# A hybrid decoder step: six feed-forward blocks regrouped into five, with the sample stages moved to the front

## The chip, the cores and the metric

The kernel runs on one core of one Trainium2 chip. The metric is the device time of one execution in microseconds (us). Weights, inputs and outputs lie in HBM; the core has TensorE (PE in the profile, with PEld for the loading of its weights), VectorE (DVE), ScalarE (ACT), GpSimd (POOL), SyncE (SP, which issues all DMAs here) and 16 DMA engines.

## The reference, cut to what matters

One layer of a decoder for 2048 prompt tokens and 64 sample tokens (8 sequences of 8), model width 1024, all in float32. Prompt and samples share the weights, but not the keys: the samples attend to caches of their own.

```
h = rmsnorm(x, g_mix);  proj = h @ w_in              # q 512, k 128, v 128, u 512
attn: causal window of 128, 8 heads on 2 kv heads, ALiBi, sinks
      (samples: keys of cache_win_k/v and the new ones)
pool: d = windowed means of u (2, 4, 8, 16) - u;  y = d @ w_pool * pool_scale
x = x + concat(attn, pool) @ w_out
h = rmsnorm(x, g_cross); q = h @ w_cq
x = x + softmax(q mem_k / 16) mem_v @ w_co           # 4 heads, 256 memory tokens
      (samples: cache_mem_k, cache_mem_v)
h = rmsnorm(x, g_ffn)
x = x + square(relu(h @ w_up)) @ w_down              # hidden 4096
y = rmsnorm(x, g_final)
```

Returned are y for prompt and samples, and the new keys, values and pooling states.

## The kernel before

Activations are kept transposed: 128 partitions of channels, tokens along the columns, so a matmul has a 128 x 128 weight tile as the stationary operand and the tokens of one block as columns. Each float32 operand is split into a rounded high part and a low rest, and each product takes three matmuls (high x high, high x low, low x high): these are L280 to L282 in `dense`, and L111 to L113 in `mm3`.

After a prologue, which normalises the 256 memory tokens, makes the memory's keys and values and folds w_cq, w_co and the pooling weights into scratch tensors in DRAM (a_s, b_s, wo_s), the program goes through three rounds, `superblock(s, ...)`, here called stage 1 to 3. Each has two token blocks (`SBLOCKS`): 384 and 384, 384 and 384, 256 and 256 + 64. The last block carries the 64 sample tokens. In each stage:

- `dense` on "in" makes k, v, q and the pooling input u for the two blocks. The first chunks ("lead") run alone; the rest is interleaved by `mix` with the window attention (`attn`). In stage 1 the lead also holds four folds (`fold`), each with two stores to wo_s through `put_fold`.
- "wo" adds the output projection to x, which `load_x` has loaded anew into XT[0] and XT[1]; these two buffers serve attention as scratch in between. `Norm` squares x on ScalarE, adds the squares on GpSimd (L206), and sums over partitions with a matmul against ones (L214, in `fin`); `apply` scales (DVE), rounds (ACT) and subtracts (DVE and POOL in turn).
- `cross` does the memory attention by the folded weights, with 512 columns of memory as moving operand. In stage 3, `mix(cross(), sample_cross(), 1, 2)` runs the samples' own attention beside it; `load_split` loads and splits w_cq and w_co there. The samples' window attention (`attn_sample`, with cache inputs cvz, ckz and spool) also runs in stage 3.
- "B" adds the memory output to x and normalises for the feed-forward (`after_co`).
- Feed-forward: `up(g)` and `down(g)` for eight groups of 512 hidden channels. up has four chunks of 24 matmuls per block and group; down has eight chunks of 12 per block and group. up(g) and down(g - 1) alternate, so the hidden activations of two groups are live. At the end `norm1` starts the next stage's first norm beside down(6) and down(7), and `final` scales and stores y.

The order on the engines follows the program's text, moved about by the framework's scheduler within the dependencies, which are tracked by the region of a buffer that an instruction touches. The calls of `flush` set when the pieces of a norm are put between the chunks of matmuls. Weight tiles come through `Stream`: a DMA of 512 KB into a staging buffer (FS, six of them), a rounding copy on ACT into WS (L132) and a subtraction on DVE (L133); up to five tiles are prepared ahead. Activations sit in 16 slots of 4 x 384 columns (ACTS), handed out in turn: four for a normalised block, two each for q, d, pt and a hidden group of one block.

Of the kernel before, what the change touches and what calls it, by code (L numbers as in the profile page):

```python
# [14 lines left out]
P = 128  # L15
# [36 lines left out]
def kernel(ctx: ExitStack, tc: tile.TileContext, io, nW=12, nF=6, nT=8):  # L52
# [8 lines left out]
    ACTS = Slots([sb(f"act{i}", 4 * NB, F32R) for i in range(16)])  # L61
    WS = Slots([sb(f"w{i}", 1024, F32R) for i in range(nW)])
    FS = Slots([sb(f"f{i}", 1088) for i in range(nF)])
    TS = Slots([sb(f"t{i}", 400) for i in range(nT)])
    XT = [sb(f"x{i}", 3136) for i in range(2)]
# [4 lines left out]
    b_s = drp.tile([8, P, 1024], F32, name="b_s", tag="b_s")  # L70

# [167 lines left out]
    class Act:  # L239
        def __init__(self, n):  # L240
            self.n = n
            self.h = [ACTS.get(), ACTS.get()]
            self.l = [ACTS.get(), ACTS.get()]

# [6 lines left out]
        def free(self):  # L251
            ACTS.put(*self.h, *self.l)
            self.h = self.l = None
# [107 lines left out]
    def prologue():  # L361
# [10 lines left out]
        hm = Act(256)  # L372
# [21 lines left out]
        for name, dst in (("ck", io["mk"]), ("cv", io["mv"])):  # L394
            a = Act(256)
# [47 lines left out]
    def make_blks(s):  # L443
        blks = []
        off = 0
        for b, (t0, npr, ns) in enumerate(SBLOCKS[s]):
            bl = Blk()
            bl.s, bl.b, bl.t0, bl.np, bl.ns, bl.n, bl.off = s, b, t0, npr, ns, npr + ns, off
            off += npr
            bl.xt = XT[b]  # L450
            bl.x = (lambda bl: lambda k, c0=0, c1=None: bl.xt[:, 0:8 * bl.n].rearrange("p (k n) -> p k n", n=bl.n)[:, k, c0:bl.n if c1 is None else c1])(bl)
            blks.append(bl)
        return blks

    def norm1(bl, wait=2):
# [5 lines left out]
        else:  # L461
            xs = [FS.get() for _ in range(4)]
            for i in range(4):
                nc.sync.dma_start(xs[i][:, 0:2 * n], io["x"][:, 8 * bl.t0 + 2 * i * n:8 * bl.t0 + 2 * (i + 1) * n])
# [4 lines left out]
        def rest():  # L469
            nm.fin()  # L470
            bl.h1 = Act(n)
# [5 lines left out]
    def load_x(bl):  # L477
        nc.sync.dma_start(bl.xt[:, 0:8 * bl.n], io["x"][:, 8 * bl.t0:8 * (bl.t0 + bl.n)])

    def superblock(s, blks, nxt):  # L480
        last = s == 2
        smp = blks[1] if last else None
# [8 lines left out]
        for bl in blks:  # L491
            bl.q = [ACTS.get(), ACTS.get()]
# [3 lines left out]
        if last:  # L496
# [14 lines left out]
        def in_evac(c, b, ps):  # L511
            bl = blks[b]
            n = bl.n
            if c == 0:
                for kv in range(2):
# [7 lines left out]
                    if b == 1 and not last:  # L523
                        for hl in range(2):
                            i = 2 * kv + hl
                            nc.gpsimd.tensor_copy(kcar[:, i * P:i * P + P], f32(kz[kv][hl][:, P + npt - P:P + npt]))
                if smp is bl:
                    t = TS.get()
                    nc.vector.tensor_copy(t[:, 0:192], ps[:, bl.np - P:n])
                    nc.sync.dma_start(io["wkp"], t[:, 0:P])  # L530
# [6 lines left out]
            elif c == 1:  # L537
                nc.vector.tensor_copy(v32[:, bl.off:bl.off + n], ps[:, 0:n])
                if smp is bl:
# [798 lines left out]
```

## Time and profile before

| | us |
|---|---|
| median of 3 runs (lowest, highest) | 2630.92 (2629.46, 2634.61) |
| the profiled execution | 2637.38 |
| its span, first to last instruction | 2635.6 |
| TensorE busy | 2570.1 |
| VectorE, ScalarE, GpSimd busy | 1305.4, 982.7, 667.5 |
| moved by DMA | 244.76 MB, 93 GB/s on average |
| granted TensorE clock | 0.991 |

In the profile a line such as "L280 PE MATMUL mm<-act,w 128\*128 128x384 f32 x1856" is a group: the source line, the engine, the operation, output and inputs by the program's names, the shape, and the count. Durations of single matmuls overlap, since they are pipelined; their pace is read from start to start. A row of the stretches gives the length, the busy time of PE, PEld, DVE, ACT and POOL, each with the instructions that touch the stretch, then the granted clock as a share of full speed, the busy share of the DMA engines, and GB/s. In a timeline, brackets hold the idle time before an instruction and what ended it.

### The profile page before, as it was taken

The numbers are of one execution on the slowest core, as the hardware profiler recorded it, in microseconds if no ns is written. First come the engines' busy times: TensorE is split into PE (matmuls) and PEld (weight loads), VectorE is DVE, ScalarE is ACT, GpSimd is POOL, SyncE is SP. The second block draws the span as 40 slices with busy tenths as digits, with TensorE's granted clock in tenths as the row PEclk, the third lists the DMA queues.
The fourth block names the chain that finished last, engine by engine and source line by source line (L and its number), as shares of the span: only waits on it lengthen the run. The fifth ranks groups of instructions, "written<-read, shape, count | busy, mean of one in ns | idle before, by whom it ended". The sixth has DMA issues, their size and how long they took to land. (4 is left out here: it accounts for less than half of the span.)

```text
span 2635.6 us, 39262 instructions
## 1 busy us (share of the span) xinstructions
PE 2570.1 (98%) x15753; PEld 2462.3 (93%) x15753; DVE 1305.4 (50%) x2283; ACT 982.7 (37%) x1923; POOL 667.5 (25%) x723
## 2 busy tenths in 40 slices
PE   8999999999999999999999999999999999999998
PEld 8799989999999999897999999999999669999998
DVE  8667553533333367936353333334766646334334
ACT  6666342422222244824342222223354434322231
POOL 2215322411111153433241111113324214111111
PEclk9999999999999999999999999999999999999999
DMA  7833111111111123131111111112414573222210
GB/s 276 262 124 117 64 47 66 65 65 64 65 65 64 56 68 109 52 125 57 67 58 61 64 64 64 65 56 69 141 61 148 179 265 110 88 81 81 87 59 37
DMA packets 92539, 244.76 MB, mean 93 GB/s; under 512 B 16772, under 2 KB 31556, under 8 KB 91204
## 3 DMA queue, kind: packets, MB, share of 16 engines
q1 hardware_dynamic: 92356, 242.25, 26.9%
q8 instruction: 123, 2.02, 0.3%
q14 instruction: 60, 0.49, 0.1%
HBM read 219.53 MB, written 22.69 MB: 92 GB/s over the span
## 5 line engine op out<-in xcount | busy, mean ns | idle before, releaser
L280 PE MATMUL mm<-act,w 128*128 128x384 f32 (+2 forms) x2784 | 904.8, 325 | 2.6 <-ACT act L631 1.6
L281 PE MATMUL mm<-act,w 128*128 128x384 f32 (+2 forms) x2784 | 899.9, 323 | 7.0 <-DVE act L235 5.6
L282 PE MATMUL mm<-act,w 128*128 128x384 f32 (+2 forms) x2784 | 898.3, 323 | 1.2 <-DVE w L133 1.2
L132 ACT CAST w<-f 128x1024 fp32r<-128x1024 f32 x330 | 346.1, 1050 | 742.2 <-PE mm L112 457.4
L133 DVE TENSOR_TENSOR w<-f,w 128x1024 fp32r<-128x1024 f32 x330 | 423.5, 1289 | 305.8 <-ACT w L132 305.5
L111 PE MATMUL mm<-act,w 128*128 128x384 f32 (+2 forms) x1728 | 552.7, 320 | 9.2 <-ACT w L132 7.5
L113 PE MATMUL mm<-act,w 128*128 128x384 f32 (+2 forms) x1728 | 548.8, 318 | 0.5 <-DVE w L133 0.5
L112 PE MATMUL mm<-act,w 128*128 128x384 f32 (+2 forms) x1728 | 549.0, 318 | 0.0
L281 PEld LDWEIGHTS mm<-act,w 128*128 128x128 f32 x2784 | 528.3, 190 | 16.5 <-DVE act L235 7.3
L280 PEld LDWEIGHTS mm<-act,w 128*128 128x128 f32 x2784 | 528.4, 190 | 7.7 <-issue 3.0
L282 PEld LDWEIGHTS mm<-act,w 128*128 128x128 f32 x2784 | 528.0, 190 | 2.0 <-DVE w L133 1.8
L1131 POOL TENSOR_TENSOR t<-t 128x384 f32<-128x384 f32 (+2 forms) x192 | 218.1, 1136 | 1039.9 <-ACT t L1130 1039.9
L1164 DVE TENSOR_TENSOR x<-mm,x 128x384 f32<-128x384 f32 (+2 forms) x384 | 199.6, 522 | 325.3 <-PE mm L113 325.3
L111 PEld LDWEIGHTS mm<-act,w 128*128 128x128 f32 x1728 | 327.1, 189 | 10.9 <-ACT w L132 7.5
L112 PEld LDWEIGHTS mm<-act,w 128*128 128x128 f32 x1728 | 327.2, 189 | 1.2 <-issue 0.3
L113 PEld LDWEIGHTS mm<-act,w 128*128 128x128 f32 x1728 | 326.9, 189 | 0.8 <-DVE w L133 0.8
L206 POOL TENSOR_TENSOR t<-t,t 128x384 f32<-128x384 f32 (+2 forms) x161 | 192.8, 1198 | 348.6 <-ACT t L205 316.1
L1134 DVE TENSOR_TENSOR act<-t,act 128x384 fp32r<-128x384 f32 (+2 forms) x192 | 102.8, 535 | 301.2 <-ACT act L1133 301.2
L1133 ACT CAST act<-t 128x384 fp32r<-128x384 f32 (+2 forms) x192 | 93.5, 487 | 236.2 <-POOL t L1131 236.1
L1130 ACT ACTIVATE t<-mm 128x384 f32<-128x384 f32 (+2 forms) x192 | 88.3, 460 | 97.1 <-PE mm L282 96.1
L205 ACT ACTIVATE t<-x 128x384 f32<-128x384 f32 (+2 forms) x140 | 68.2, 498 | 143.7 <-DVE x L1093 66.4
L111 PE MATMUL mm<-w,act 128*128 128x512 f32 x288 | 116.1, 405 | 2.9 <-ACT w L132 2.9
(187 smaller groups left out, 2209.9 us busy)
## 6 DMA issues: line engine op xcount, KB each, us to landing
f<-in_wup SPq DMA_DIRECT2D x96, 512.0 KB, 3.5
f<-in_wdn SPq DMA_DIRECT2D x96, 512.0 KB, 3.5
f<-in_win SPq DMA_DIRECT2D x30, 512.0 KB, 3.7
f<-a_s SPq DMA_DIRECT2D x24, 512.0 KB, 3.4
f<-b_s SPq DMA_DIRECT2D x24, 512.0 KB, 4.5
x<-in_x SPq DMA_DIRECT2D x6, 1536.0 KB, 7.8
f<-in_wco SPq DMA_DIRECT2D x16, 512.0 KB, 5.2
f<-in_cmk SPq DMA_DIRECT2D x16, 512.0 KB, 4.5
```

What stands on the lines that cost most here:

```text
L111: nc.tensor.matmul(ps, Wh(k), Hh(k), start=first and i == 0, stop=False)
L112: nc.tensor.matmul(ps, Wh(k), Hl(k), start=False, stop=False)
L113: nc.tensor.matmul(ps, Wl(k), Hh(k), start=False, stop=final and i == last)
L132: nc.scalar.copy(th[:], r[:, 0:1024])
L133: eng.tensor_tensor(tl[:], r[:, 0:1024], f32(th[:]), ALU.subtract)
L206: self.add.tensor_tensor(self.acc[:, 0:n], self.acc[:, 0:n], t[:, 0:n], ALU.add)
L280: nc.tensor.matmul(ps[:, 0:n], w8(th)[:, k, :], hi(b, k), start=k == 0, stop=False)
L281: nc.tensor.matmul(ps[:, 0:n], w8(th)[:, k, :], lo(b, k), start=False, stop=False)
L282: nc.tensor.matmul(ps[:, 0:n], w8(tl)[:, k, :], hi(b, k), start=False, stop=k == 7)
L1131: nc.gpsimd.tensor_tensor(q[:, 0:n], r[:, 0:n], r[:, 0:n], ALU.mult)
L1134: nc.vector.tensor_tensor(lo, q[:, 0:n], f32(hi), ALU.subtract)
L1164: nc.vector.tensor_tensor(bl.x(m), ps[:, 0:n], bl.x(m), ALU.add)
```

## The change

The prompt is cut anew: stage 1 has 256 prompt tokens and 256 + 64 samples, stages 2 and 3 have twice 384. So the samples' attention, pooling and memory attention move from stage 3 to stage 1. In stage 1 the feed-forward runs over the two prompt blocks as one block of 512 columns (`merged`), except up(0) and down(7), which stay at 256 per block. The samples' x is stored after the memory attention (xs_s, in DRAM), and 16 of its columns are loaded with each of the four later blocks, whose feed-forward and final norm run over 400 columns.

The 16 activation slots become four groups of four (h0, h1, q0, q1), each one buffer that the feed-forward views in units of 512 or 400 columns instead. With 400 columns 16 units don't fit into one group: the last one comes from a staging buffer (for the normalised input) or from a cp buffer (for hidden). `load_split` takes its pair from the group that has the most free slots.

```
 SBLOCKS = [
-    [(0, 384, 0), (384, 384, 0)],
-    [(768, 384, 0), (1152, 384, 0)],
-    [(1536, 256, 0), (1792, 256, 64)],
+    [(0, 256, 0), (256, 256, 64)],
+    [(512, 384, 0), (896, 384, 0)],
+    [(1280, 384, 0), (1664, 384, 0)],
 ]
+NX = [256, 320, 400, 400, 400, 400]
+NY = [256, 256, 400, 400, 400, 400]
...
-    ACTS = Slots([sb(f"act{i}", 4 * NB, F32R) for i in range(16)])
+    BIG = {g: sb(f"act{g}", 16 * NB, F32R) for g in ("h0", "h1", "q0", "q1")}
+    ACT = {g: Slots([t[:, 4 * NB * i:4 * NB * (i + 1)] for i in range(4)]) for g, t in BIG.items()}
+    GH = [ACT["h0"], ACT["h1"]]
+    GQ = [ACT["q0"], ACT["q1"]]
...
     def load_x(bl):
...
+            nc.sync.dma_start(bl.xv[:, :, 0:bl.n], src.rearrange("p (k n) -> p k n", n=bl.n))
+            j = 2 * (bl.s - 1) + bl.b
+            nc.sync.dma_start(bl.xv[:, :, bl.n:NM], xs_s[:].rearrange("p (k n) -> p k n", n=64)[:, :, 16 * j:16 * j + 16])
...
-        smp = blks[1] if last else None
+        smp = blks[1] if s == 0 else None
...
+            if smp and (c, b) == (0, 0):
+                nc.sync.dma_start(X1[:, 0:2048], io["ckz"])
+                nc.gpsimd.memset(X1[:, 2048:3136], 0.0)
...
         def load_split(src):
-            r, th, tl = FS.get(), ACTS.get(), ACTS.get()
+            G = max(GQ + GH, key=lambda g: len(g.free))
+            r, th, tl = FS.get(), G.get(), G.get()
...
+            nc.sync.dma_start(xs_s[:].rearrange("p (k n) -> p k n", n=64), bl.xv[:, :, bl.np:bl.n])
...
+            if merged:
+                if b == 0:
+                    for G in GH:
+                        ml.take += [(G, G.get()) for _ in range(4)]
+                c = slice(256 * b, 256 * b + 256)
+                h3 = lambda k: ml.h3[k][:, c]
+            else:
+                ml.take += [(GH[b], GH[b].get()) for _ in range(4)]
+                if b == 0:
+                    ml.f = FS.get()
...
+        merged = s == 0
...
         def up(g):
-            run(dense([("up", s, g, c) for c in range(4)], blks,
-                      lambda b, k: blks[b].h3.hi(k), lambda b, k: blks[b].h3.lo(k), up_evac(g),
-                      head=4 if g == 0 else 0, tail=0))
+            if merged and g:
+                for c in range(4):
+                    th, tl = S.next(("up", s, g, c))
+                    ps = MM.get()
+                    mm3(ps[:], range(8), lambda k: w8(th)[:, k, :], lambda k: w8(tl)[:, k, :],
+                        lambda k: ml.h3[k], lambda k: ml.h3[8 + k])
+                    WS.put(th, tl)
+                    f = FS.get()
+                    relu2(ps, hidu(0, g, c), hidu(0, g, 4 + c), 512, f[:, 0:512], f[:, 512:1024])
+                    FS.put(f)
+                    MM.put(ps)
+                    flush()
+                return
...
         def down(g):
...
-            seq = [(mp, b) for b in ends for mp in range(4)] if fin else [(mp, b) for mp in range(4) for b in range(2)]
+            both = merged and not fin
+            seq = [(mp, b) for b in ends for mp in range(4)] if fin else [(mp, b) for mp in range(4) for b in range(1 if both else 2)]
...
-                    nc.vector.tensor_tensor(bl.x(m), ps[:, 0:n], bl.x(m), ALU.add)
+                    if both:
+                        for x in blks:
+                            nc.vector.tensor_tensor(x.x(m), ps[:, 256 * x.b:256 * x.b + 256], x.x(m), ALU.add)
+                    else:
+                        nc.vector.tensor_tensor(bl.x(m), ps[:, 0:n], bl.x(m), ALU.add)
                     MM.put(ps)
                     if fin:
                         bl.norm.sq(m)
+                    if both and m2 == 0:
+                        flush()
```

More of the change, by code (lines that the diff above doesn't have):

```diff
@@ L854, in attn @@
                         units.append(u)
-            if last:
+            if smp:
                 yield from attn_sample()
@@ L900, in after_out @@
             bl.norm.fin()
-            ACTS.put(*bl.q, *bl.d)
-            bl.h2 = Act(bl.n)
-            yield from bl.norm.apply(V_GCROSS, bl.h2.hi, bl.h2.lo, 8 if last and b else PIECE[1][b])
+            GQ[b].put(*bl.q, *bl.d)
+            bl.h2 = Act(bl.n, GH[b])
+            yield from bl.norm.apply(V_GCROSS, bl.h2.hi, bl.h2.lo, 8 if smp and b else PIECE[1][b])
         for bl in blks:
@@ L1173, in down @@
                     later.append([DEFF[bl.b], lambda bl=bl: final(bl)])
-            for b in range(2):
-                ACTS.put(*hid.pop((g, b)))
         def final(bl):
@@ L1191, in superblock @@
                 down(g - 1)
-        for bl in blks:
-            bl.h3.free()
+        for G, t in ml.take:
+            G.put(t)
+        if not merged:
+            FS.ids.discard(id(ml.f))
+            f = pool.tile([P, 1088], F32, name=f"{ml.ft}f{s}", tag=ml.ft)
+            ftag[id(f)] = ml.ft
+            keep.append(f)
+            FS.ids.add(id(f))
+            FS.put(f)
         S.resF = 4 if nxt is not None else 0
@@ L1200, in superblock @@
         down(7)
-    TS2 = [sb(f"cp{i}", 512) for i in range(2)]
     vcarry = [None]
```

148 lines of the change are left out of this document (91 added, 57 removed).

## The prediction

> **What bounds the kernel now.** I read the page first, then the busy time by stretch, then the timeline of TensorE in a few places, the waits of TensorE, and last the DMA issues.
>
> ```profile
> span 2635.6 us, 39262 instructions
> PE 2570.1 (98%) x15753; PEld 2462.3 (93%) x15753; DVE 1305.4 (50%) x2283; ACT 982.7 (37%) x1923; POOL 667.5 (25%) x723
> 600.00:900.00 300.00, 300.00 (x1732) 300.00 (x1731) 105.46 (x148) 69.31 (x102) 38.39 (x33) 1.00 0.19 63
> 2172.00:2196.00 24.00, 24.00 (x202) 24.00 (x201) 11.16 (x15) 8.46 (x14) 9.10 (x10) 1.00 0.55 200
> 2300.00:2600.00 300.00, 300.00 (x2248) 300.00 (x2247) 118.22 (x188) 82.09 (x137) 46.63 (x46) 1.00 0.20 69
> ...
> 357.58 0.40 PE L113 MATMUL mm<-w,act 128*128 128x512 f32 x1
> ...
> 362.36 0.39 PE L113 MATMUL mm<-w,act 128*128 128x512 f32 x1
> ```
>
> Columns of the stretches: length, busy us of PE, PEld, DVE, ACT, POOL (instructions), granted clock, DMA share, GB/s. TensorE is the bound: 98% busy, and without a gap in the feed-forward, where the other engines are at most 40% busy. So the change is worth what it takes from TensorE's stream, less the gaps that it opens.
>
> The stretches give the pace from start to start. 600 to 900 lies in the first feed-forward, all 384 columns: 300/1732 = 173.2 ns. 2172 to 2196 has 256 columns: 24/202 = 118.8, or 120 if the two cut at the ends are left out; I take 119.5. 2300 to 2600 is the last feed-forward, 256 and 320 in turn: 300/2248 = 133.4 on average. The two timeline rows are the 3rd and the 24th matmul of a 512-column group: 4.78/21 = 227.6. A line through 384 and 512 has (227.6 - 173.2)/128 = 0.425 ns per column, and leaves 173.2 - 163.2 = 10 ns that don't depend on columns; through 256 and 384 it is 0.42 and 12. Per matmul some 11 ns are fixed. That is all the change can save.
>
> **The feed-forward.** One block has 1536 matmuls: 32 up chunks and 32 down chunks of 24. Six blocks are 9216. Afterwards block 1 and 2 are one of 512 columns, except the first up group and the last down group, which stay at 256 each: 2 x 192 = 384 matmuls of 256, and 7 x 96 + 7 x 96 = 1344 of 512. Four blocks of 400 have 6144. The columns add up to the same 1536 x 2112; 1344 matmuls fall away.
> Before: 6144 x 173.2 ns + 3072 x 133.4 ns = 1064.1 + 409.8 = 1473.9 us. After, with 173.2 + 16 x 0.425 = 180.0 for 400 columns: 384 x 119.5 ns + 1344 x 227.6 ns + 6144 x 180.0 ns = 45.9 + 305.9 + 1105.9 = 1457.7. Saved: 16.2 us; with a fixed part of 10 to 13 ns, 13 to 17.5.
> The Trainium skill (TensorE: Matmul & The Clock Gate, "Wait — 56ns, not 53.3ns?") gives a start-to-start of N / 2.4 GHz plus about 2.5 ns for warm matmuls in bf16; by it, as an estimate, 1344 x 2.5 = 3.4 us would be saved. The rows here, with a weight load before each matmul, show four times that fixed part.
>
> Other engines in the merged stage: a chunk of 24 lasts 24 x 227.6 = 5.5 us (before, two blocks, 8.3 us) and needs one weight tile.
>
> ```profile
> L133 DVE TENSOR_TENSOR w<-f,w 128x1024 fp32r<-128x1024 f32 x330 | 423.5, 1289 | 305.8 <-ACT w L132 305.5
> L132 ACT CAST w<-f 128x1024 fp32r<-128x1024 f32 x330 | 346.1, 1050 | 742.2 <-PE mm L112 457.4 <-PE mm L281 243.5 <-DMA f<-in_wco 10.1
> L1131 POOL TENSOR_TENSOR t<-t 128x384 f32<-128x384 f32 x128 | 150.9, 1179 | 752.8 <-ACT t L1130 752.8
> f<-in_wup SPq DMA_DIRECT2D x96, 512.0 KB, 3.5
> ```
>
> Cast 1.05, subtraction 1.29, the square on POOL 1.18 x 512/384 = 1.6, a landing of 3.5 us: all under 5.5, so at nothing. The 400-column evacuations grow by 4% under the same cover, and the staging buffer that the last feed-forward unit borrows leaves five for tiles needed every 24 x 2 x 0.18 = 8.6 us: nothing.
>
> **The tail.** The program now ends on 400 columns, not 256.
>
> ```profile
> 2624.08 0.28 PE L113 MATMUL mm<-act,w 128*128 128x256 f32 x1
> 2624.37 1.07 DVE L1164 TENSOR_TENSOR x<-mm,x 128x256 f32<-128x256 f32 x3
> 2625.29 1.56 PE L198 MATMUL aux<-t,ones 128*128 128x256 f32 x6 [0.93 <-ACT t L195]
> 2626.89 0.47 ACT L217 ACTIVATE t<-aux,eps 128x256 f32<-128x256 f32 x1 [0.99 <-PE aux L198]
> 2629.30 3.26 DVE L1181 SCALAR_TENSOR_TENSOR x<-x,vec,t 128x256 f32<-128x256 f32 x8
> L1181 DVE SCALAR_TENSOR_TENSOR x<-x,vec,t 128x384 f32<-128x384 f32 x32 | 18.6, 649 | 0.1
> L217 ACT ACTIVATE t<-aux,eps 128x384 f32<-128x384 f32 x16 | 9.2, 572 | 11.8 <-PE aux L214 11.8
> L198 PE MATMUL aux<-t,ones 128*128 128x256 f32 x16 | 5.0, 411 | 0.9 <-ACT t L195 0.9
> ```
>
> L1181 grows from 3.26/8 = 0.41 to about 0.58 apiece (18.6/32 at 384): +1.4. The five small operations of the norm grow as L217 does, from 0.47 to 0.57 at 384, so by some 0.13 each: +0.7. The 16 norm matmuls go six in 1.56 us, at about 0.215 each; by 400/256 that is 0.335: +1.9. Against it the three adds that stood in a row after the last matmul (they had queued behind the other block's final scaling) shrink to one, since a chunk now covers more: -0.7. Sum +3.3 (2 to 5).
>
> **The start.** Some 0.8 MB of x less (192 columns of 4 KB) is loaded and normalised in the prologue (256 and 320 columns, not twice 384), but the sample inputs come here: cvz, ckz and spool, 2.25 MB.
>
> ```profile
> 77.33 1.21 PE L214 MATMUL aux<-t,ones 128*128 128x384 f32 x2 [2.62 <-POOL t L206]
> 90.00:105.00 15.00, 14.24 (x66) 11.30 (x66) 9.05 (x11) 10.86 (x19) 4.87 (x3) 1.00 0.88 271
> 105.00:118.00 13.00, 11.16 (x42) 8.71 (x41) 3.68 (x3) 6.95 (x10) 0.00 (x0) 0.87 1.01 321
> 118.00:130.00 12.00, 11.95 (x64) 10.71 (x62) 6.74 (x11) 8.82 (x16) 0.00 (x0) 1.00 0.74 238
> 130.00:145.00 15.00, 14.73 (x81) 14.15 (x82) 8.87 (x12) 9.01 (x14) 1.17 (x4) 1.00 0.87 272
> f<-in_cvz SPq DMA_DIRECT2D x2, 512.0 KB, 3.8
> x<-in_ckz SPq DMA_DIRECT2D x1, 1024.0 KB, 9.4
> x<-in_spool SPq DMA_DIRECT2D x1, 240.0 KB
> f<-in_wop SPq DMA_DIRECT2D x4, 512.0 KB, 4.7
> wo_s<-f SPq DMA_DIRECT2D x8, 256.0 KB, 2.6
> ```
>
> The wait of 2.62 us for the second block's squares shrinks with 320 columns: -2 (-4 to 0). From 90 to 145 the DMA engines are 0.74 to 1.01 busy, and TensorE already waits there (11.16 of 13.00 busy, clock 0.87). 2.25 MB at 271 GB/s are 8.3 us of all engines, put on SP ahead of the weight tiles that the input projection needs next; the room up to 145 is 15 x 0.12 + 12 x 0.26 + 15 x 0.13 = 6.9 us. SP also holds: the store of the old keys reads ckz, so SP stands until it has landed (9.4 us), with weight loads queued behind it. Bounds: 0 (prefetched tiles cover it) to +12 (most of the 8.3 us and a cold clock). I take +6, as the stretch is nearly full. The same transfers leave stage 3; the row of 1890 to 1900 in the next part shows TensorE busy throughout beside them, at a DMA share of 0.65, so I count no gain there.
>
> **Moved and shortened joints.** The sample stage itself keeps its instructions and its partner shape (256 and 320), so its small waits move with it at nothing.
>
> ```profile
> PE aux L214 <- POOL t L206: 13.4, 9, 2.6
> 1889.29 0.91 PE L214 MATMUL aux<-t,ones 128*128 128x384 f32 x2 [2.55 <-POOL t L206]
> 1890.00:1900.00 10.00, 10.00 (x64) 9.96 (x63) 8.54 (x16) 3.73 (x7) 0.00 (x0) 0.83 0.65 175
> 1013.11 0.91 PE L214 MATMUL aux<-t,ones 128*128 128x384 f32 x2 [1.26 <-POOL t L206]
> 934.00:1003.00 69.00, 69.00 (x394) 68.10 (x393) 49.55 (x70) 29.95 (x55) 38.86 (x35) 1.00 0.26 84
> ```
>
> Stage 3 now opens with 384-column chunks, as stage 2 does: its final norm waits 1.26, not 2.55, and the cold clock behind it (0.83 over 10 us, 1.7 us) goes: -3. The joint of stage 1 and 2 tightens: its last two down groups last 8 x 2.73 + 192 x 0.1195 = 44.8 us, not 69. In these POOL has 38.9 us of work, less some 14 x 0.4 for shorter final squares; the next blocks' norms must be ready in 44.8. 33 in 44.8 fits, but late adds can hold the norm matmul: +2 (0 to 8).
>
> Sample cross-attention loads w_cq and w_co through pairs of activation slots. Before, all 16 slots rotated and 6 or 7 were free: three pairs. Now slots are tied to a group of four: two pairs.
>
> ```profile
> L961 ACT CAST act<-f 128x1024 fp32r<-128x1024 f32 x16 | 16.7, 1049 | 9.1 <-DMA f<-in_wco 5.0 <-PE aux L113 2.4 <-PE mm L282 1.6
> L962 DVE TENSOR_TENSOR act<-f,act 128x1024 fp32r<-128x1024 f32 x16 | 20.0, 1262 | 7.7 <-ACT act L961 7.0
> ```
>
> Cast 1.05, subtraction 1.26 and six matmuls 1.37 make 3.7 us, some 4.0 with hand-overs; with two pairs 2.0 us per tile against 1.4 of TensorE. Sixteen tiles: up to +9, down to 0 where other matmuls fill in. +3.
> The four extra loads of 16 sample columns and the store of xs are not needed for a whole attention stage: nothing, with 0.6 for SP.
>
> Sum: -16.2 + 3.3 - 2 + 6 - 3 + 2 + 3 + 0.6 = -6.3 us. It is made against the profiled execution, 2637.4 us with a span of 2635.6; the median of the runs is 2630.9, 6.5 lower, and I apply the difference to that: 2624.6, rounded 2624.5. Some 0.2%, 5.3 us, is what can be told from no change here.
>
> **Rivals.**
> 1. The gain arrives nearly whole: the early loads and the sample weights are covered, joints too. -16.2 + 3.3 - 2 - 3 = -17.9: 2613. For it: prefetch of up to five tiles; against: the DMA share of 0.87 to 1.01.
> 2. The start eats it: the lead loses 12 to 16 us, not 6. +0 to +4: 2631 to 2635, no change. For it: the 2.25 MB sit in the one full stretch of the program.
> 3. Slower: staging buffers. Of six, v takes one and cvz two, so three carry the lead's 10 tiles and 8 fold stores. A tile holds one for 4.7 + 1.05 + 1.29 = 7.0 us, a store for about 2.6 + 2: 107 us, or 36 per buffer, against 35 us of TensorE's work there (72 x 0.1195 + 144 x 0.147 + 24 x 0.2276). If only two turn at a time it is 53: a stall of 18 and a cold clock of 2 to 3 in place of my 6, so +9: 2640. It decides from a stall of 17.6 us (6 + 6.3 + 5.3). Against it: several of these tiles are loaded before the lead starts.
> 4. Fewer matmuls save less than the line says: if most of the fixed part lies under the weight load before each matmul and stays when columns are merged, say 3 ns of 11 go, 1344 x 3 = 4 us are saved and the sum is +5.9: 2637. Four widths on one line speak against it. The Trainium skill's rule quoted above comes to nearly this time.
>
> **Chances.** The forecast (2619 to 2630) 0.43, rival 1 0.26, rival 2 0.17, rival 3 0.10, rival 4 0.04. Faster by over 0.2%, below 2625.6: rival 1 and 0.28 of the forecast, 0.54. Within: the rest of the forecast, and most of rival 2, 0.29. Slower, 0.17. The range 2611 to 2638 leaves out rival 3 and the edges; the forecast's own is 2619 to 2630.
>
> **What would show it.** L280 to L282 and L111 to L113 at 400 columns at 180 ns from start to start, and 1344 fewer matmuls; waits of L280 to L282 for L133 or L132 before 160 us, some 6 us; the norm matmul (L214 before) at the opening of stage 3 waiting 1.3 us at most; a tail 3 us longer; in stage 1, TensorE waiting for the split of w_cq and w_co (the lines that were L961 and L962). It is wrong if the lead's waits are over 18 us, or if the pace at 400 or 512 columns isn't on the line.

## The result, and the profile after

The changed kernel takes 2658.2 us (median of four runs, 2655.5 to 2660.2) against 2632.8 us for the kernel before on the same chip: a ratio of 1.0095, 95% interval 1.0077 to 1.0113. It is slower by some 25 us, where the prediction had it faster by 6. The profiled execution took 2660.15 us, 22.8 more than that of before. In what follows, a ratio is always to runs of the kernel before beside it on the same chip, and 0.1% is 2.6 us. One execution of the run with early wpool, at a granted clock of 0.556 (4207 us), is left out of that run's median and ratio. Lines have moved by eleven or so: L122 to L124 are `mm3`, L291 to L293 `dense`, L143 and L144 the rounding and splitting of weight tiles, L225 the norm's matmul, L217 its adds on GpSimd.

From the page of the changed kernel and its busy time by stretch (columns as before):

```profile
PE 2576.7 (97%) x14409; PEld 2407.6 (91%) x14409; DVE 1298.3 (49%) x2256; ACT 974.8 (37%) x1867; POOL 658.9 (25%) x695
```

```profile
118.00:130.00 12.00, 5.41 (x40) 5.14 (x38) 6.05 (x11) 4.94 (x10) 1.60 (x6) 0.84 0.83 250
130.00:145.00 15.00, 9.09 (x28) 7.30 (x29) 3.67 (x6) 5.71 (x10) 0.00 (x0) 0.61 0.78 203
145.00:160.00 15.00, 12.52 (x65) 11.38 (x65) 5.16 (x8) 5.84 (x8) 0.00 (x0) 0.84 0.64 213
600.00:750.00 150.00, 150.00 (x664) 124.24 (x663) 65.42 (x100) 43.88 (x55) 22.25 (x14) 1.00 0.28 99
1300.00:1600.00 300.00, 300.00 (x1649) 300.00 (x1648) 100.90 (x137) 71.60 (x107) 42.86 (x37) 1.00 0.18 62
```

and the last of these stretches' counterpart in the lead before, which the prediction did not show:

```profile
145.00:160.00 15.00, 14.71 (x87) 14.35 (x86) 6.96 (x14) 5.71 (x10) 0.00 (x0) 1.00 0.54 187
```

There are 1344 matmuls fewer, as counted, and yet TensorE is busy 7 us longer. Two things are seen at once. First, the lead: from 118 to 160 us TensorE is busy 27.0 of 42 us; before it was 41.4 of 42. The idle time grew by 14.4 us, and what ran there ran at a granted clock of 0.61 to 0.84, not 1.00: busy time by missing clock gives 5.41 x 0.16 + 9.09 x 0.39 + 12.52 x 0.16 = 6.4 us more, so some 20 us were lost. Second, the pace: 512 columns take 150/663 = 226.2 ns, a little better than forecast, but 400 columns take 300/1648 = 182.0 ns, not 180.0. Over 6144 matmuls that is 12 us. The width is off the line that 256, 384 and 512 columns lie on.

The timeline of the changed kernel shows SyncE's queue in the lead, and the waits of TensorE in the lead and at the joints:

```profile
122.58 2.02 SPq L522 DMA_DIRECT2D f<-in_cvz  x2
124.69 0.38 SPq L351 DMA_DIRECT2D f<-in_wpool  x1
...
133.69 1.66 SPq L344 DMA_DIRECT2D wo_s<-f  x2
135.45 0.45 SPq L142 DMA_DIRECT2D f<-in_win  x1
...
131.34 0.80 PE L122 MATMUL mm<-w,w 128*128 128x512 f32 x1 [7.93 <-ACT w L354]
140.75 0.58 PE L291 MATMUL mm<-acth,w 128*128 128x256 f32 x1 [4.10 <-ACT w L143]
785.77 0.91 PE L225 MATMUL aux<-t,ones 128*128 128x384 f32 x2 [1.84 <-POOL t L217]
811.30 0.91 PE L225 MATMUL aux<-t,ones 128*128 128x384 f32 x2 [2.49 <-POOL t L217]
1746.64 0.94 PE L225 MATMUL aux<-t,ones 128*128 128x400 f32 x2 [1.36 <-POOL t L217]
```

In the kernel before, the same two loads stand in SyncE's queue so:

```profile
122.29 0.35 SPq L340 DMA_DIRECT2D f<-in_wpool  x1
122.73 0.38 SPq L131 DMA_DIRECT2D f<-in_win  x1
```

The first fold waits 7.93 us for wpool's rounding (L354). wpool is issued behind the two loads of cvz, 2.4 us later than before, and takes 6.1 us to land, not 2.7. The second in-projection tile is issued at 135.45, behind stores and 12.7 us later than before, and TensorE waits 4.10 us for it. At the joint of stage 1 and 2 both norms wait for GpSimd's adds. The opening of stage 3 waits 1.36 us.

### The profile page after: what moved, and what is told of

The parts are those of the page before. It is cut to its first block, busy times and chain, and to the rows that moved or that the text cites. A ratio compares the mean times of both kernels' runs of the same rounds, so it can differ in the third digit from the quotient of the medians.

```text
span 2658.3 us, 36411 instructions
## 1 busy us (share of the span) xinstructions
PE 2576.7 (97%) x14409; PEld 2407.6 (91%) x14409; DVE 1298.3 (49%) x2256; ACT 974.8 (37%) x1867; POOL 658.9 (25%) x695
## 4 chain that ended last, share of the span: by engine, by line
PE 80%; DVE 8%; ACT 4%; POOL 3%; DMA 3%; issue 2%; SPq 0%; DVEq 0%; ACTq 0%; POOLq 0%
PE mm L124 13%; PE mm L122 13%; PE mm L123 13%; PE mm L292 13%; PE mm L293 12%; PE mm L291 12%; DVE t L243 3%; DVE w L144 1%; POOL t L217 1%; ACT w L143 1%; PE aux L699 1%; DVE acth L246 1%; POOL t L617 1%; ACT x L711 1%; PE aux L730 1%
## 5 line engine op out<-in xcount | busy, mean ns | idle before, releaser
L143 ACT CAST w<-f 128x1024 fp32r<-128x1024 f32 x311 | 325.9, 1050 | 693.3 <-PE mm L123 470.0
L144 DVE TENSOR_TENSOR w<-f,w 128x1024 fp32r<-128x1024 f32 x311 | 393.3, 1269 | 302.8 <-ACT w L143 298.4
L291 PE MATMUL mm<-acth,w 128*128 128x400 f32 (+3 forms) x1568 | 532.6, 340 | 6.6 <-ACT w L143 5.9
L293 PE MATMUL mm<-acth,w 128*128 128x400 f32 (+3 forms) x1568 | 529.4, 338 | 1.2 <-DVE w L144 1.2
L292 PE MATMUL mm<-acth,w 128*128 128x400 f32 (+3 forms) x1440 | 486.8, 338 | 6.1 <-DVE acth L246 5.4
L122 PE MATMUL mm<-actq,w 128*128 128x400 f32 (+2 forms) x1376 | 478.2, 348 | 1.1 <-ACT f L342 1.1
L124 PE MATMUL mm<-actq,w 128*128 128x400 f32 (+2 forms) x1376 | 478.7, 348 | 0.0
L123 PE MATMUL mm<-actq,w 128*128 128x400 f32 (+2 forms) x1248 | 433.5, 347 | 0.0
L1178 POOL TENSOR_TENSOR t<-t 128x400 f32<-128x400 f32 (+1 forms) x136 | 163.1, 1200 | 812.3 <-ACT t L1177 812.3
L291 PEld LDWEIGHTS mm<-acth,w 128*128 128x128 f32 x1568 | 298.1, 190 | 10.1 <-ACT w L143 6.8
L293 PEld LDWEIGHTS mm<-acth,w 128*128 128x128 f32 x1568 | 299.2, 191 | 1.7 <-DVE w L144 1.7
L1239 DVE TENSOR_TENSOR x<-mm,x 128x400 f32<-128x400 f32 (+1 forms) x272 | 152.9, 564 | 281.6 <-PE mm L124 278.6
L292 PEld LDWEIGHTS mm<-acth,w 128*128 128x128 f32 x1440 | 273.9, 190 | 11.2 <-DVE acth L246 7.3
L217 POOL TENSOR_TENSOR t<-t,t 128x384 f32<-128x384 f32 (+3 forms) x161 | 191.2, 1188 | 351.7 <-ACT t L216 348.3
L122 PEld LDWEIGHTS mm<-actq,w 128*128 128x128 f32 x1376 | 259.5, 189 | 11.7 <-ACT f L342 1.5
L124 PEld LDWEIGHTS mm<-actq,w 128*128 128x128 f32 x1376 | 260.8, 190 | 9.5
L291 PE MATMUL mm<-actq,w 128*128 128x384 f32 (+2 forms) x768 | 248.0, 323 | 0.8 <-DVE x L915 0.6
L293 PE MATMUL mm<-actq,w 128*128 128x384 f32 (+2 forms) x768 | 246.2, 321 | 2.0 <-DVE w L144 2.0
L292 PE MATMUL mm<-actq,w 128*128 128x384 f32 (+2 forms) x768 | 246.5, 321 | 0.0
L123 PEld LDWEIGHTS mm<-actq,w 128*128 128x128 f32 x1248 | 235.4, 189 | 9.9
L1180 DVE TENSOR_TENSOR actq<-t,actq 128x400 fp32r<-128x400 f32 (+1 forms) x120 | 71.1, 593 | 222.1 <-ACT actq L1179 222.0
L291 PEld LDWEIGHTS mm<-actq,w 128*128 128x128 f32 x768 | 145.6, 190 | 3.3 <-DVE x L915 0.9
```

Source lines behind the costliest of these rows:

```text
L122: nc.tensor.matmul(ps, Wh(k), Hh(k), start=first and i == 0, stop=False)
L123: nc.tensor.matmul(ps, Wh(k), Hl(k), start=False, stop=False)
L124: nc.tensor.matmul(ps, Wl(k), Hh(k), start=False, stop=final and i == last)
L143: nc.scalar.copy(th[:], r[:, 0:1024])
L144: eng.tensor_tensor(tl[:], r[:, 0:1024], f32(th[:]), ALU.subtract)
L217: self.add.tensor_tensor(self.acc[:, 0:n], self.acc[:, 0:n], t[:, 0:n], ALU.add)
```

## The experiments

**The lead: buffers or transfers?** The first edit takes cvz's two staging buffers, and loads them, behind the lead (e7, e9 and e10 below keep this edit); the second takes the buffers where the changed kernel does, and moves the two transfers alone. In this and the later cuts from the edits, calls are shortened.

```
             cvs = [FS.get(), FS.get()]                 # e1 moves this line, too
-            for i in range(2): dma_start(cvs[i], cvz)
...
         S.resW = RW                                    # the text of the lead ends here
+            for i in range(2): dma_start(cvs[i], cvz)  # e1 and e2
```

> The changed kernel with one edit: cvz's two staging buffers are taken, and its two loads issued, after the lead of stage 1 and not ahead of it; ckz and spool stay early. In the changed kernel TensorE waits 7.9 us for wpool and 4.1 us for an in-projection tile in the lead, beside a clock down to 0.61 for 15 us, some 20 us lost against the kernel before. Theory A (too few staging buffers: v one, cvz two of six, so the weight loads are issued late) expects five buffers to turn in the lead, wpool to be issued some 6 us earlier, the 7.9 and 4.1 us waits to shrink below 2 us and the clock to stay at 0.9 or more: 14 to 19 us less than the changed kernel, 2639 to 2644. Theory B (the 2.25 MB on the DMA engines and on SP's queue ahead of the weights, buffers not scarce) expects only the 1 MB of cvz to be out of the way: 5 to 10 us, 2648 to 2653. Theory C (the lead's loss has another cause, such as ckz or the stores of the sample keys) expects 3 us at most.

> The changed kernel with one edit: cvz's two staging buffers are taken ahead of the lead as in the changed kernel, but its two loads are issued after the lead. So the buffers are as scarce as in the changed kernel, and the transfers are out of the way. Theory A (too few staging buffers) expects the lead's waits to stay, 2653 to 2659. Theory B (transfers and queue ahead of the weights) expects what the late cvz alone gives, 2639 to 2653, the same as the run with late buffers within 3 us. Part of each would show as a time half-way.

Late cvz: 2650.8 us, ratio 1.0063 (1.0050 to 1.0076), 0.32% or 8 us below the changed kernel. Buffers held, transfers late: 2660.9, 1.0101 (1.0087 to 1.0115), no gain. The lead's three stretches, of the first and then of the second:

```profile
118.00:130.00 12.00, 6.58 (x41) 5.87 (x40) 7.23 (x15) 5.55 (x14) 1.61 (x6) 0.82 0.61 185
130.00:145.00 15.00, 13.39 (x66) 11.56 (x65) 4.74 (x6) 8.01 (x11) 0.00 (x0) 0.80 0.92 276
145.00:160.00 15.00, 15.00 (x105) 14.78 (x104) 8.87 (x14) 7.18 (x12) 0.00 (x0) 1.00 0.78 259
```

```profile
118.00:130.00 12.00, 6.06 (x42) 5.56 (x40) 6.31 (x13) 6.34 (x15) 1.40 (x6) 0.85 0.69 194
130.00:145.00 15.00, 11.86 (x48) 10.20 (x47) 3.67 (x7) 4.52 (x7) 0.21 (x1) 0.66 0.83 229
145.00:160.00 15.00, 9.76 (x43) 7.78 (x42) 4.62 (x7) 5.46 (x8) 0.00 (x0) 0.79 0.76 229
```

Idle time is 7.0 us in the first and 14.3 in the second, against 15.0: freeing the buffers gains 8 us, moving the transfers without them nothing. The second run is not as clean a test as its expectation has it, since its two loads are issued in the middle of the lead, not behind it:

```profile
133.31 0.65 SPq L865 DMA_DIRECT2D f<-in_cvz  x1
139.15 0.54 SPq L865 DMA_DIRECT2D f<-in_cvz  x1
```

With them out of its way wpool lands in 3.2 us, not 6.1, and the first fold waits 5.94 us, not 7.93: the megabyte did cost that fold some 2 us. What eats this gain is further back: the last weight tile of the folds (wop) is issued at 144.77, in the changed kernel at 143.31, with late cvz at 135.80. SyncE's waits from 118 to 165 us show how long weight loads stand for a store of the folds to land, in the changed kernel, then with late cvz, then with buffers held:

```profile
SPq L142 <- DMA wo_s<-f: 6.2, 2, 4.9
```

```profile
SPq L142 <- DMA wo_s<-f: 2.2, 2, 1.9
```

```profile
SPq L142 <- DMA wo_s<-f: 6.8, 2, 4.3
```

The numbers are us in all, times, longest: a weight load that waits for such a store needs its staging buffer. So the larger part is the buffers. But with late cvz the lead still has only 6.58 of 12 us in its first row, and its first fold still waits 5.42 us. A part of the loss is something else.

**The rest of the lead.** Three edits, each on top of late cvz: wpool loaded ahead of the last quarter of the prologue's folds; ckz and the store of the old keys put behind the lead as well; the four folds put behind the 4th to 7th chunk.

```
+            if h == 2: S.resW = 1                   # e7: in the prologue
+            if h == 3: S.wpr = prep_fold()
-                nc.sync.dma_start(X1, io["ckz"])    # e9: behind the lead
-            if s == 0 and m < 4:     fold(m, wpr)
+            if s == 0 and 3 <= m < 7: fold(m - 3, wpr)   # e10
```

> The kernel with the late cvz (2650.8 us, a wait of 5.4 us for wpool and a clock of 0.80 from 130 to 145 us) with one more edit: wpool's buffer, load and rounding come before the last quarter of the prologue's folds, not behind them. Theory A (wpool is late because its issue stands in SP's order behind the stores of b_s and waits for a buffer, while the two in-projection chunks that covered it became shorter: 256 and 320 columns for twice 384) expects the wait to go and the clock to stay up: 5 to 9 us less, 2642 to 2646. Theory B (the transfers themselves bound the lead, DMA being 0.9 busy) expects the wait to move to the next tile, of the in-projection or of w_out: 2 us less at most.

> The kernel with the late cvz (2650.8 us) with one more edit: ckz's load and the store of the old keys come behind the lead, too, so 1 MB in and 1 MB out less stand in SP's order and on the DMA engines ahead of the lead's weights. Theory B (transfers in front of the weights hold the rest of the lead's loss) expects the 5.4 us wait for wpool to fall below 3 and 3 to 6 us less, 2645 to 2648. Theory F (the rest comes from the two shortened in-projection chunks that used to cover the folds' first operands: 24 matmuls of 256 and 24 of 320 for 48 of 384, 1.9 us less cover, and no buffer or transfer) expects the wait to stay and 2 us less at most.

> The kernel with the late cvz (2650.8 us) with one more edit: the four folds come after the 4th to 7th chunk of the in-projection, not after the 1st to 4th, and their weights stand in that order in the stream. Theory F (the cover of the folds' operands became too short) expects the wait for wpool to go, since 12.8 us of chunks stand ahead of the first fold, and 4 to 8 us less, 2643 to 2647. Theory B (loads bound the lead) expects the wait to go over to the in-projection's second tile, and 2 us less at most.

Early wpool: 2650.0, 1.0064 (1.0046 to 1.0082), nothing gained over late cvz (1.0063). wpool is issued at 117.41, not 124.17, but takes 8.2 us to land, not 2.8, and the first fold still waits 5.38 us; its buffer is now missing to the prologue's stores, of which the last is issued at 127.71. Late ckz: 2651.6, 1.0066 (1.0053 to 1.0080), nothing. Late folds: 2647.2, 1.0050 (1.0036 to 1.0064), 0.13% or 3 us better than late cvz, with the intervals overlapping; the trace is clearer, with 3.9 us of idle time in the three stretches, not 7.0. Its first two stretches, and the wait that is left:

```profile
118.00:130.00 12.00, 12.00 (x88) 11.82 (x87) 8.02 (x17) 6.17 (x15) 1.60 (x6) 1.00 0.67 193
130.00:145.00 15.00, 11.12 (x62) 9.97 (x61) 6.94 (x10) 8.84 (x12) 0.00 (x0) 0.89 0.75 248
```

```profile
134.08 0.39 PE L291 MATMUL mm<-acth,w 128*128 128x256 f32 x1 [3.41 <-ACT w L143]
```

The wait for wpool is gone, so its cover was short: 24 matmuls of 256 and 24 of 320 columns stand where 48 of 384 stood. But 3.41 of those 5.42 us come back as a wait for the in-projection's third tile, much as theory B said: each theory has its part.

A third way to free buffers leaves cvz and the folds where the changed kernel has them, and lets the two evacuations of a fold share one staging buffer:

```
-            put_fold(ps, ...)                       # a buffer for each half
+            if eh == 0: o = FS.get()
+            nc.scalar.copy(o[:, 512*eh:512*eh+512], ps[:])
+            nc.sync.dma_start(wo_s[...], o[:, 512*eh:512*eh+512])   # b_s alike
```

> The changed kernel with one edit: the two evacuations of a fold into b_s or wo_s share one staging buffer (they fill half of one each), so the folds need half as many; cvz stays early. Theory A (staging buffers are what the lead lacks) expects the waits of 7.9 and 4.1 us there to fall by half or more, and 6 to 12 us less than the changed kernel, 2646 to 2652. Theory B (cvz's buffers alone, which leave three, or transfers) expects less than 3 us, as a shared buffer is held longer by its two stores.

2650.4 us, 1.0055 (1.0041 to 1.0069), 0.40% or 10 us less than the changed kernel. The lead's three stretches:

```profile
118.00:130.00 12.00, 6.86 (x30) 5.73 (x29) 5.34 (x12) 6.37 (x16) 0.59 (x2) 0.80 0.83 294
130.00:145.00 15.00, 11.42 (x60) 9.20 (x59) 5.00 (x10) 5.20 (x8) 2.02 (x4) 0.84 0.77 215
145.00:160.00 15.00, 14.96 (x91) 13.85 (x91) 8.20 (x11) 8.62 (x12) 0.00 (x0) 0.87 0.90 254
```

Idle time is 8.8 us, not 15.0, with cvz still issued ahead of the lead, at 118.64. It is buffers again, by another door. The lead also starts 3.4 us earlier, at 113.42, as the prologue's stores share buffers, too, so a part of the 10 us may come from there.

**The pace at 400 columns.** In the first run the 400-column units start every 384 columns, in the second 384-column matmuls start every 400. The first, and the third with four distances, let units overlap and so compute with wrong values; the second leaves out the samples' feed-forward.

```
-    u = [BIG[f"h{b}"][:, NM*i:NM*i+NM] ...]             # starts 1600 bytes apart
+    u = [BIG[f"h{b}"][:, UO(i):UO(i)+NM] ...]           # e3: 1536 (e5: four distances)
-    n = 400;  +    n = 384                              # e4, starts left at 1600
```

> The changed kernel with one edit: the 400-column units of activations in the feed-forward of stages 2 and 3 start every 384 columns (1536 bytes), where the 384-column units of the kernel before started, not every 400 (1600 bytes). The units overlap, so the 16 sample columns of these blocks hold wrong data; the instructions and their number are the same. In the changed kernel a 400-column matmul takes 182.2 ns from start to start on average, between 176.5 and 187 by its place in the chunk, against 180.0 by the line through the other widths. Theory A (the start address of the moving operand costs time where it isn't a multiple of 512 bytes) expects 180.0 ns at all places, 6144 x 2.1 = 13 us less: 2645. Theory B (the width of 400 itself costs it) expects 182.2 ns and 2658.

> The changed kernel with one edit: in the feed-forward of stages 2 and 3 the matmuls and what follows them take 384 of the 400 columns, from units that still start every 400 columns. The samples' feed-forward is left out by this. Theory A (start address) expects 384 columns to pay the same 2 ns as 400 do, 175.4 ns against 173.2 in the kernel before: 6144 x (182.2 - 175.4) = 42 us less than the changed kernel, 2616. Theory B (the width of 400) expects 173.2 ns: 55 us less, 2603.

> The changed kernel with one edit: the distance between the starts of the 400-column units is 352 columns (1408 bytes, 11 x 128) in the up matmuls of stage 2, 336 (1344 bytes, 21 x 64) in the down matmuls of stage 2, 320 (1280 bytes, 5 x 256) in the up matmuls of stage 3 and 328 (1312 bytes, 41 x 32) in the down matmuls of stage 3. Units overlap, so the feed-forward of these stages computes with wrong data; instructions and their number are the same. With starts every 1536 bytes a 400-column matmul took 180.0 ns, with 1600 bytes (25 x 64) 182.2 ns. Theory A (a start must be a multiple of 128 bytes) expects 180.0, 182.2, 180.0 and 182.2 or more. Theory B (a multiple of 256) expects 181 or more, 182.2, 180.0, 182.2 or more. Theory C (a multiple of 512) expects more than 180.0 in all four. Theory D (64 bytes are enough, and 1600 bytes were slow for another reason, such as where the units lie to each other) expects 180.0 in the first three.

Stretch from 1300 to 1600 us of the first, then of the second:

```profile
1300.00:1600.00 300.00, 300.00 (x1668) 300.00 (x1667) 102.91 (x141) 71.05 (x105) 41.35 (x35) 1.00 0.18 62
```

```profile
1300.00:1600.00 300.00, 300.00 (x1715) 300.00 (x1715) 104.35 (x145) 70.97 (x106) 40.73 (x35) 1.00 0.19 64
```

400 columns now take 300/1667 = 180.0 ns, 384 columns take 300/1714 = 175.0 in place of 173.2: it is the start, not the width. The times are 2651.0 (1.0059, 1.0045 to 1.0073), 9 us below the changed kernel, and 2618.6 (0.9939, 0.9925 to 0.9952). The third run tells which starts are good. Between the first matmul of one group of 192 and that of the next (down then up in stage 2, with distances of 1344 and 1408 bytes; down then up in stage 3, with 1312 and 1280; lines lie two further down in this kernel):

```profile
1246.77 0.35 PE L124 MATMUL mm<-actq,w 128*128 128x400 f32 x1
1281.76 0.34 PE L293 MATMUL mm<-acth,w 128*128 128x400 f32 x1
1316.75 0.35 PE L124 MATMUL mm<-actq,w 128*128 128x400 f32 x1
...
2153.47 0.34 PE L124 MATMUL mm<-actq,w 128*128 128x400 f32 x1
2188.45 0.34 PE L293 MATMUL mm<-acth,w 128*128 128x400 f32 x1
2223.01 0.34 PE L124 MATMUL mm<-actq,w 128*128 128x400 f32 x1
```

34.99, 34.99, 34.98 and 34.56 us over 192 are 182.2, 182.2, 182.2 and 180.0 ns (one execution, 2661.6 us). Only the distance of 5 x 256 bytes is free; 11 x 128 is not. Theory B holds. The remedy with nothing left out starts the units every 448 columns (7 x 256 bytes), which costs four of twelve weight buffers in these feed-forwards:

```
+    w = WS.get()
+    u = [BIG[f"h{b}"][:, 448*i:448*i+NM] for i in range(13)] + [fx, w[:, 0:], w[:, 512:]]
```

> The changed kernel with one edit, nothing left out: the 400-column units of the feed-forward of stages 2 and 3 start at multiples of 256 bytes, every 448 columns. 13 of 16 fit into a group; the others take a staging or cp buffer as before and two places in a weight buffer, so four of the twelve weight buffers are gone in these feed-forwards. If the starts are the cause of 182.2 ns, 400 columns take 180.0 ns, and 6144 x 2.15 = 13 us go: 2645. If four prepared tiles fewer starve TensorE, waits for the rounding of weights appear in the feed-forward and less than 8 us go.

2647.5 us, 1.0059 (1.0044 to 1.0074): 0.36% or 9 us back. In its trace the feed-forward runs at 300/1668 = 179.9 ns, without waits:

```profile
1300.00:1600.00 300.00, 300.00 (x1669) 300.00 (x1668) 103.24 (x140) 71.03 (x105) 41.29 (x35) 1.00 0.19 62
```

**The merging itself.** Stage 1's feed-forward at 256 columns throughout:

```
-            if merged and g:
+            if False:            # and both = False in down
```

> The changed kernel with one edit: the feed-forward of stage 1 runs at 256 columns per block throughout, not at 512. That brings back the 1344 matmuls that the merging takes away. If the fixed part of a matmul is what 256 and 512 columns show (2 x 119.5 - 226.5 = 12.5 ns), this takes 16.8 us more than the changed kernel, 2675. If matmuls beside a weight load of their own save little by merging (3 ns each), it takes 4 us more, 2662. If the wider blocks also cost something elsewhere in stage 1 (their adds, the borrowed staging buffers for the squares), it takes less than either.

```profile
600.00:750.00 150.00, 150.00 (x1252) 150.00 (x1252) 62.79 (x102) 46.82 (x82) 27.77 (x28) 1.00 0.29 92
```

2676.2 us, 1.0158 (1.0140 to 1.0175), 0.63% or 17 us more than merged. 256 columns take 150/1251 = 119.9 ns, so a merged pair saves 2 x 119.9 - 226.2 = 13.6 ns. The gain that the change was to bring is there.

**The joint of stage 1 and 2.** First the place of the norm's matmul is moved by a pair of chunks; then, instead, the squares of the 512-column chunks leave the staging buffers, and the second norm's adds leave GpSimd.

```
+        wait = wait or (3 if bl.s == 1 else 2)                       # e8
-                    f = FS.get()                                     # e13
+                    f = cp.get()
+            nm = Norm(..., add=nc.vector if bl.s == 1 and bl.b == 1 else None)
```

> The changed kernel with one edit: at the joint of stage 1 and 2 the sum over partitions of the next stage's norm is put three chunk pairs after its start, not two. In the changed kernel these matmuls wait 1.84 and 2.49 us for the adds on GpSimd, since a pair of chunks there is shorter than before (512 or 256 columns for twice 384). Theory A (only the place is too early) expects both waits to fall below 0.5 us and 3 to 5 us less than the changed kernel, 2653 to 2655. Theory B (the norm is late as a whole) expects the wait to move to the first in-projection chunks of stage 2, and no more than 1 us less.

> The changed kernel with two edits at the joint of stage 1 and 2: the squares of the 512-column chunks use two cp buffers that are idle there, in place of a staging buffer per chunk, and the squares of the second norm are added on VectorE, not on GpSimd. Theory A (the first norm is late because the loads of x wait for staging buffers that the wide squares hold, the second because 10 adds of 1.17 us stand in a row on GpSimd) expects the two waits of 1.8 to 3 us to fall below 1 us, and 3 to 5 us less than the changed kernel, 2653 to 2655. Theory B (a joint of 45 us is too short for the two norms whatever their buffers) expects the waits to stay above 1.5 us or to move on, and less than 2 us.

Moved: 2658.6, 1.0089 (1.0075 to 1.0102), no change that can be told. The waits moved on by some 17 us each, to a down chunk at 802.83 and to the first in-projection chunk of stage 2 at 828.53, which wait 3.11 and 2.73 us for VectorE's adds of a down product.

Freed: 2653.1, 1.0062 (1.0048 to 1.0075), 5 us by the medians, 9 by the ratios. In the changed kernel the second norm's adds were one row on GpSimd; with the edits the first wait is gone and of the second 0.61 us are left:

```profile
801.86 11.70 POOL L217 TENSOR_TENSOR t<-t,t 128x384 f32<-128x384 f32 x10
```

```profile
806.55 0.91 PE L225 MATMUL aux<-t,ones 128*128 128x384 f32 x2 [0.61 <-DVE t L217]
```

With the edits the first loads of x, which the first norm needs, are issued earlier. In the changed kernel, then with the edits:

```profile
764.32 8.54 SPq L477 DMA_DIRECT2D f<-in_x  x3
```

```profile
747.25 16.65 SPq L477 DMA_DIRECT2D f<-in_x  x4
```

The two edits were not run apart on the changed kernel. But the first version of the next part has the VectorE adds without the cp buffers, and there the first norm still waits, and the second less:

```profile
773.07 0.91 PE L225 MATMUL aux<-t,ones 128*128 128x384 f32 x2 [2.92 <-POOL t L217]
797.59 0.91 PE L225 MATMUL aux<-t,ones 128*128 128x384 f32 x2 [1.53 <-DVE t L217]
```

By these traces the first norm was late by its buffers and the second by them and by GpSimd's row of adds, not because 45 us are too short.

**All together.** The first version has late cvz and ckz, late folds, aligned units and VectorE adds; the second late cvz, late folds, paired stores, aligned units (given back one group earlier), and both edits at the joint. The last run gives the kernel before the paired stores alone.

> The changed kernel with all remedies, nothing left out: cvz, ckz and the store of the old keys behind the lead, folds after the 4th to 7th chunk, units at multiples of 256 bytes, and the squares of stage 2's second block added on VectorE at the joint. If each pays as its own cause says (8 for the buffers, 4 to 8 for the folds, 13 for the starts, 0 to 3 each for ckz and the adds) it takes 2624 to 2633, at or just below the kernel before. If the lead is bound by transfers, it stays at 2636 to 2640.

> The changed kernel with all that helped, nothing left out: cvz behind the lead, folds after the 4th to 7th chunk, fold stores in pairs, units at multiples of 256 bytes (the extra places in weight buffers given back one chunk group earlier), and the joint of stage 1 and 2 with cp buffers and VectorE adds. From the run with late cvz and late folds (2647) less 10 to 13 for the starts, 3 for the joint and 0 to 5 for the pairs: 2626 to 2634, against 2633 to 2636 for the kernel before. If it stays over 2632 there is no version here that beats the kernel before by more than can be told.

> The kernel before (six blocks) with one edit: the two evacuations of a fold share one staging buffer, as in the fastest version. If the kernel before has buffers enough in its lead (11.95 of 12.00 and 14.73 of 15.00 us busy there), it stays within 2 us of 2634, and the fastest version owes its 11 us to the regrouped feed-forward with its repairs. If the pairs shorten the prologue's waits for the stores of b_s (1 to 2 us each at three places), it gains 2 to 4 us. If the shared buffers are held longer, it loses 1 to 3.

The first: 2633.7, 0.9996 (0.9986 to 1.0006), level with the kernel before, at the slow edge of what was expected. The second: 2624.7 us, 0.9954 (0.9940 to 0.9968), some 12 us faster than the kernel before. Its stretches:

```profile
118.00:130.00 12.00, 10.31 (x72) 9.77 (x71) 8.18 (x17) 6.57 (x15) 2.46 (x5) 1.00 0.87 279
130.00:145.00 15.00, 11.88 (x71) 10.62 (x70) 8.11 (x16) 8.79 (x13) 0.98 (x2) 0.92 0.86 253
145.00:160.00 15.00, 15.00 (x90) 14.76 (x89) 7.34 (x15) 5.89 (x10) 0.00 (x0) 0.85 0.86 254
```

The lead is idle for 4.8 us, not 15.0. The kernel before with paired stores: 2634.9, 0.9991 (0.9981 to 1.0001), the same within what can be told. So the fastest version does not owe its gain to the paired stores as such. Its other edits were not tried on the kernel before, which has little for them to win: 0.6 us of idle time in these three stretches, and 1.26 us of wait at the joint. That the gain is the regrouped feed-forward's, once its side costs are paid back, is argued from this, and from the 17 us that the merging saves, and not shown by a run.

## Why the prediction was wrong, step by step

| step | predicted, us | found, us |
|---|---|---|
| merging to 512 columns | -16.2, with the next row | -17 (run without it) |
| 400 columns at 180.0 ns | on the line | +12 by the pace, +9 by the runs |
| tail | +3.3 | +1.8 |
| second norm of the prologue | -2 | -1.5 (1.14 for 2.62) |
| lead of stage 1 | +6 (0 to 12) | some +20, by the trace |
| opening of stage 3 | -3 | as predicted |
| joint of stage 1 and 2 | +2 (0 to 8) | +5 to +9 |
| sample cross-attention, two pairs | +3 (0 to 9) | 0 |

With the 0.6 for SyncE the found terms sum to +15 to +22; the profiled executions differ by 22.8, so up to 8 us stay unassigned.

**The merging** was right in kind and size: the fixed part per matmul is what the line through the widths said, 12 to 14 ns. Rival 4, a saving of 4 us, is refuted by the run without merging (17 us). The Trainium skill's start-to-start rule for bf16 (TensorE: Matmul & The Clock Gate, "Wait — 56ns, not 53.3ns?") has a fixed part of about 2.5 ns; the 13.6 ns measured here, with a weight load before each matmul, do not agree with it.

**The step that failed most is the lead.** The prediction priced 2.25 MB of transfers against the free room of the DMA engines at +6, and put the staging buffers at nothing in its sum; it named them only in rival 3, at a chance of 0.10. Transfers moved alone gained no time: cvz with its buffers held (2660.9 against 2658.2), ckz and the store of the old keys (2651.6 against 2650.8). Freed buffers gained 8 and 10 us. Rival 3 had the mechanism of the larger part, and nearly the size (a stall of 18 us and 2 to 3 of cold clock; measured 15 and 6, with the second cause below in it). What it was set against, that several tiles are loaded before the lead, holds for three of its ten, issued at 108.29 and 114.48; wpool and the second in-projection tile are issued at 124.69 and 135.45, into the lead. And the term had a second, smaller cause that no part of the prediction held: the lead's first two chunks shrank from 384 columns to 256 and 320, while every load and store beside them stayed. The prediction had the lead's 35 us of TensorE work, but did not set it against the work of the same place before. The cold clock stands beside the waits: 7.93 and 4.10 us, and a granted clock of 0.61 from 130 to 145 us. The Trainium skill (TensorE: Matmul & The Clock Gate, "HAM oscillation — how this bites in real kernels") says that gaps over about 3.4 us bring the clock to half. The trace agrees.

**The pace at 400 columns** was taken from a line through widths whose units all started at multiples of 256 bytes. It holds exactly, 180.0 ns, where they do. The diff shows the starts (`NM * i`); the prediction read the width and not the address, and the term is missing from its sum and its rivals.

**The joint** was named, with its wait and its engine; mis-sized by 3 to 7 us. Most of that is in the waits of 1.84 and 2.49 us, where before there was one of 1.26. The prediction's 33 us of GpSimd work in 44.8 us counted the mean, while ten adds came in one row, and it did not count that the wide squares hold staging buffers that x's loads need.

**Tail, prologue and stage 3** came as written, the tail a little shorter. Two rows of the timeline of the changed kernel:

```profile
74.80 0.81 PE L225 MATMUL aux<-t,ones 128*128 128x320 f32 x2 [1.14 <-POOL t L217]
...
2644.95 0.35 PE L124 MATMUL mm<-actq,w 128*128 128x400 f32 x1
```

From the last product's matmul to the end of the span it is 2658.3 - 2644.95 = 13.35 us; before it was 2635.6 - 2624.08 = 11.52. **The sample cross-attention** cost nothing more: the waits for the split of w_cq and w_co are 1.6 us in all, 1.7 before. From the waits of TensorE in the changed kernel, then in that of before:

```profile
PE aux L123 <- DVE acth L986: 0.9, 2, 0.5
PE aux L123 <- DVE actq L986: 0.7, 1, 0.7
```

```profile
PE aux L112 <- DVE act L962: 1.5, 2, 0.8
PE aux L111 <- ACT act L961: 0.2, 1, 0.2
```

The numbers are us in all, times, longest. With two pairs where there were three, nothing is late.

## What to carry to other kernels

When a stage is moved to another place, count what it holds (buffers, for how long) beside what it transfers, and set the work that covers each load before against that after, chunk by chunk: a shorter chunk is a shorter cover. A line through known sizes prices a new size only if the new operands also lie as the old ones did, so read the starts in the diff, not the shapes alone. And a wait that moves when its place is moved is not cured: look for the buffer or the queue behind it.

## What was not expected of the hardware

A 400-column float32 matmul (with a weight load before each) takes 180.0 ns from start to start when its moving operand's units start at multiples of 256 bytes of their buffer (distances of 1536 and 1792 bytes, and 1280 in one execution), and 182.2 ns on average when they lie 1600 bytes apart (or 1408, 1344 or 1312, in that one execution); 384 columns at 1600 bytes pay 175.0 for 173.2. It is 1% of a busy TensorE, and 9 to 12 us of this kernel. Why 128 bytes are not enough was not tried.
